# 172 products of the identity with itself, put into TensorE's queue in three places of a two-layer decoder

## The chip, the core and the metric

The kernel runs on one core of a Trainium2 chip. What counts is the device time of one execution in microseconds (us): the median over the runs. A core has a TensorE (matrix products and transposes, called PE in the profile, with PEld for its weight loads), a VectorE (DVE), a ScalarE (ACT), a GpSimd (POOL) and a SyncE (SP), which here issues most of the DMAs. Each engine takes its instructions from a queue of its own, in order; semaphores make one wait for another. TensorE runs at one of two levels, 1.2 or 2.4 GHz; the profile gives the granted clock as a share of the full one, 0.50 or 1.00, and something between for a stretch in which it changed.

## The reference

Two layers over 1024 tokens of width 1024, in float32. Each layer normalizes its input, projects it once into the inputs of four mixers (latent attention, a gated linear recurrence, a diagonal state space model called S5, sparse attention), puts their outputs together, projects, and adds the result to the input. A mixture of 16 experts follows, of which each token uses two:

```
for l in range(DEPTH):
    h = rms_norm(x, mix_norm[l])
    c_q, c_kv, k_pe, lru_x, lru_gate, s5_u, nsa_q, nsa_kv, nsa_gate = jnp.split(h @ w_in[l], IN_SPLITS, axis=-1)
    ...                                   # the four mixers: y_a, y_b, y_c, y_d
    y = rms_norm(jnp.stack([y_a, y_b, y_c, y_d], axis=2), out_norm[l]).reshape(x.shape)
    x = x + y @ w_out[l]
    x = x + hier_moe(rms_norm(x, ffn_norm[l]), ...)   # route, then the experts' gated MLPs

def rms_norm(x, g): return x * rsqrt(mean(x * x, -1) + EPS) * g
```

`hier_moe` picks the best of four groups for a token and the two best of the four experts in it; each expert is `silu(t @ w_gate) * (t @ w_up)` times `w_down`, weighted and summed.

## The kernel before, in words

A matrix product of float32 is made of three products of rounded parts (`mm3`, lines 179 to 183: high by high, high by low, low by high); `hi` (line 169) makes the high part on ScalarE and `lo` (line 177) the low part on VectorE. PSUM, where TensorE writes, has eight banks of 128 x 512 float32; `pt` hands out four of them under names: two called t, one called o, one called x. A bank is given out again when the last reader of its former tile is done.

A layer runs through these stages.

*The norm* (`mixer_norm`). The tokens come in eight tiles of 128. SP loads a tile (line 448) into one of four buffers, of which one holds the gain; so the load of tile i + 3 waits until tile i is read. ScalarE squares and sums it (line 211), GpSimd makes the inverse root (lines 200 and 202), VectorE scales the tile in place (line 454), and TensorE transposes it in eight pieces of 128 x 128 (`T`, line 214), four into bank o and four into bank x. ScalarE and VectorE read each bank as high and low parts (169, 177) into `hT`, which the projection uses.

*The input projection* (`mixer_in`): seven pieces of 128 columns of the weight, each by two halves of 512 tokens, each 24 products of 512 columns, lines 181 to 183. A half needs the norm of its four tiles only. Weights are loaded and split in `wunit` (line 188 and on). In layer 1 the first four weight units are loaded behind the first three tiles.

*Mixers and output projection.* The last stage of it, for the last tile of tokens, uses banks x and o (read by VectorE in line 1510), stores the sum, transposes it and makes the 20 routing logits (line 1533, 20 columns each).

*The routing* (`router`). VectorE finds each token's group and experts (lines 1575 to 1592) and writes them as a 0/1 matrix `Mb`; TensorE turns it into each token's place in its experts' lists (`pos`, 1595 and 1598) and the counts (`cnt`, 1602), two banks t. VectorE copies the counts (1604) and makes the places (1629). Then `moe` starts: `slot_list` (1793 to 1806) finds the tokens of the first expert with 16 small products (line 1796), GpSimd gathers them (1817), TensorE transposes them (`expert_in`). Meanwhile VectorE ranks the experts by count and GpSimd writes a table of slots for all other experts with 16 indirect DMAs (`slot_table`, line 1731), which need the rows that VectorE makes in line 1726.

*The experts* (`moe`): 16 in turn; products with the up weights (into other banks), then with the down weights into banks o and x, and an indirect DMA that adds the result to the layer's output (line 1888). A branch (1936, 1937) runs more tiles if some expert has more tokens than its slots; in these inputs it isn't taken. Layer 1's norm loads what those DMAs have added.

What sets the order: `layer` is a hand-made weave of generators. From its program order, the framework's planner makes one queue for each engine when the kernel is built; it puts an instruction where it reckons that the engine is free and the operands and the bank are there, so that later lines can stand ahead of earlier ones. Nothing crosses the branch of line 1937. At run time each queue is fixed.

The change touches `mixer_norm`, `router` and `layer`, and adds `warm` to the helpers. `identb` is the 128 x 128 identity in bfloat16, made at the start (line 226).

Of the kernel before, what the change touches and what calls it, by code (L numbers as in the profile page):

```python
# [38 lines left out]
def row_bcast(ap, n):  # L39
    return bass.AP(tensor=ap.tensor, offset=ap.offset, ap=[[0, 128], [1, n]])  # L40
# [62 lines left out]
class Trunk:  # L103
# [104 lines left out]
    def meansq(self, src, n, acc, out=None):  # L208
        if out is None:
            out = self.junk()[:src.shape[0], :src.shape[1]]  # L210
        self.nc.scalar.activation(out, src, AF.Square, scale=float(n) ** -0.5, accum_out=acc)

    def T(self, out, in_, k=128):
        self.nc.tensor.transpose(out, in_, self.ident[:k, :k])  # L214
# [221 lines left out]
    def mixer_norm(self, l, src):  # L436

        nc = self.nc
        hTh, hTl = [], []
        for k in range(2):  # L440
            for a, t in (("h", hTh), ("l", hTl)):
                t.append([self.hp.tile([128, 4, 512], F32R, name=f"hT{a}{k}{j}") for j in range(2)])
        self.hT = (hTh, hTl)
        grow = self.p4(name="grow")
        nc.sync.dma_start(grow, row_bcast(self.I["mix_norm"][l], D))
        for i in range(NT):
            xt = self.p4(name="xt")
            nc.sync.dma_start(xt, src[i * 128:(i + 1) * 128, :])
            if i == 2:
                yield  # L450
            ss = self.sm(1, name="ss")
            self.meansq(xt, D, ss, self.p2((128, 1024), BF, name="sqx"))
            r = self.rsqrt(ss, 1)
            nc.vector.scalar_tensor_tensor(xt, xt, r, grow, op0=ALU.mult, op1=ALU.mult)
            for k2 in range(2):
                pt = self.pt("ox"[k2])
                for k in range(4):
                    self.T(pt[:, k * 128:(k + 1) * 128], xt[:, (4 * k2 + k) * 128:(4 * k2 + k + 1) * 128])
                p3 = pt.rearrange("p (k t) -> p k t", k=4)
                ts = slice(128 * (i % 4), 128 * (i % 4) + 128)  # L460
                hh = hTh[i // 4][k2][:, :, ts]
                self.hi(hh, p3)
                self.lo(hTl[i // 4][k2][:, :, ts], p3, hh)
# [1104 lines left out]
    def router(self, l):  # L1568
        nc, v, mp = self.nc, self.nc.vector, self.mp
        self.rtp = None  # L1570
        bc = lambda a, shp, d: a.unsqueeze(d).to_broadcast(shp)
        lg = self.LG[:, :, 0:4]
        le = self.LG[:, :, 4:20].rearrange("p i (g j) -> p i j g", g=4)
        gm = self.rt("gm", 8)
        v.reduce_max(gm, lg, axis=AX.X)
        og = self.first_max(lg, gm, "og")
        big = self.rt("big", 128)
        b4 = big.rearrange("p (i j g) -> p i j g", i=NT, j=4)
        v.tensor_tensor(b4, le, bc(og, [128, NT, 4, 4], 2), op=ALU.mult)
        lx = self.rt("lx").rearrange("p (i j) -> p i j", j=4)  # L1580
        v.reduce_sum(lx, b4, axis=AX.X)
        m1, m2 = self.rt("m1", 8), self.rt("m2", 8)
        v.reduce_max(m1, lx, axis=AX.X)
        o1 = self.first_max(lx, m1, "o1")
        lx2 = self.rt("lx2").rearrange("p (i j) -> p i j", j=4)
        v.scalar_tensor_tensor(lx2, o1, -BIG, lx, op0=ALU.mult, op1=ALU.add)
        v.reduce_max(m2, lx2, axis=AX.X)
        o2 = self.first_max(lx2, m2, "o2")
        o12 = self.rt("o12").rearrange("p (i j) -> p i j", j=4)
        v.tensor_tensor(o12, o1, o2, op=ALU.add)  # L1590
        Mb = mp.tile([128, 128], BF, name="Mb")
        v.tensor_tensor(Mb.rearrange("p (i g j) -> p i g j", i=NT, g=4), bc(og, [128, NT, 4, 4], 3),
                        bc(o12, [128, NT, 4, 4], 2), op=ALU.mult)
        pos, cnt = self.pt(), self.pt()
        nc.tensor.matmul(pos[:, 0:128], self.tri, Mb, start=True, stop=False)
        for i in range(NT - 1):
            n = NT - 1 - i
            nc.tensor.matmul(pos[:, 16 * i + 16:128].rearrange("p (i e) -> p i e", i=n), self.onesb,
                             Mb[:, 16 * i:16 * i + 16].unsqueeze(1).to_broadcast([128, n, 16]),
                             start=False, stop=i == NT - 2)  # L1600
        for i in range(NT):
            nc.tensor.matmul(cnt[:, 0:16], self.onesb, Mb[:, 16 * i:16 * i + 16], start=i == 0, stop=i == NT - 1)
        cn = self.rt("cn", 16)
        v.tensor_copy(cn, cnt[:, 0:16])

        g_ = nc.gpsimd
        t = self.rt("pgt")
        t3 = t.rearrange("p (i g) -> p i g", g=4)
        v.tensor_tensor(t3, lg, bc(gm, [128, NT, 4], 2), op=ALU.subtract)
        nc.scalar.activation(t, t, AF.Exp)  # L1610
        w = [self.rt("w1", 8), self.rt("w2", 8)]
        v.tensor_tensor(w[1], m2, m1, op=ALU.subtract)
        nc.scalar.activation(w[1], w[1], AF.Exp)
        M = []
        for k, o in enumerate((o1, o2)):
            mk = self.rt(f"M{k}", 128)
            g_.tensor_tensor(mk.rearrange("p (i g j) -> p i g j", i=NT, g=4), bc(og, [128, NT, 4, 4], 3),
                             bc(o, [128, NT, 4, 4], 2), op=ALU.mult)
            M.append(mk)
        pg = self.rt("pg", 8)  # L1620
        v.reduce_sum(pg, t3, axis=AX.X)
        den = self.rt("den", 8)
        v.scalar_tensor_tensor(den, w[1], 1.0, pg, op0=ALU.add, op1=ALU.mult)
        v.reciprocal(w[0], den)
        v.tensor_tensor(w[1], w[1], w[0], op=ALU.mult)

        self.PM = mp.tile([128, NT, 16], F32, name="PM")
        PM = self.PM.rearrange("p i e -> p (i e)")
        v.scalar_tensor_tensor(PM, pos[:, 0:128], 1.0, Mb, op0=ALU.add, op1=ALU.mult)
        v.tensor_scalar(PM, PM, -1.0, None, op0=ALU.add)  # L1630

        n = FIXED
        M3 = [m.rearrange("p (i e) -> p i e", e=16)[:, :, 0:n] for m in M]
        WC3, t3 = [self.rt(nm, NT * n).rearrange("p (i e) -> p i e", e=n) for nm in ("WC", "WT")]
        g_.tensor_tensor(WC3, M3[0], bc(w[0], [128, NT, n], 2), op=ALU.mult)
        g_.tensor_tensor(t3, M3[1], bc(w[1], [128, NT, n], 2), op=ALU.mult)
        g_.tensor_tensor(WC3, WC3, t3, op=ALU.add)
        self.split_info(0, n, WC3)

        def rank():  # L1640
            self.slot_table(l, *self.router_rank(cn), cn, M, w)
        return rank
# [311 lines left out]
    def layer(self, l, src):  # L1954
# [15 lines left out]
        if l == 0:  # L1970
            gen = self.s5_gen(0, True)
            next(gen)
        units = self.mixer_in(l)

        norm = self.mixer_norm(l, src)
        next(norm)
# [162 lines left out]
```

## Time and profile before

| | |
|---|---|
| median of 3 runs | 2172.72 us (2164.47 to 2176.85) |
| the profiled execution | 2167.18 us, of it the span of the trace 2165.4 us |
| TensorE (PE) busy | 1846.2 us, 85% of the span, 10386 products |
| weight loads (PEld) | 1508.0 us, 70% |
| VectorE (DVE) | 1309.8 us, 60% |
| ScalarE (ACT) | 1129.7 us, 52% |
| GpSimd (POOL) | 669.0 us, 31% |
| mean granted clock of TensorE | 0.899 |

Products overlap in the pipeline, and the profile counts a product as busy until its result is out; so 85% isn't the share of time in which the array works at its peak. A duration of 390 ns stands for a product of 512 columns whose successor starts 230 ns later. For a price the starts of neighbours are better than durations. The profile's chain of waits is followed back from the end to 1446 us only; it does not reach the first layer or the boundary between the layers. Layer 0 runs to 1117 us, layer 1 from there.

### The profile page before, as it was taken

The numbers are of one execution on the slowest core, as the hardware profiler recorded it, in microseconds if no ns is written. First come the engines' busy times: TensorE is split into PE (matmuls) and PEld (weight loads), VectorE is DVE, ScalarE is ACT, GpSimd is POOL, SyncE is SP. The second block draws the span as 40 slices with busy tenths as digits, with TensorE's granted clock in tenths as the row PEclk, the third lists the DMA queues.
The fourth block names the chain that finished last, engine by engine and source line by source line (L and its number), as shares of the span: only waits on it lengthen the run. The fifth ranks groups of instructions, "written<-read, shape, count | busy, mean of one in ns | idle before, by whom it ended". The sixth has DMA issues, their size and how long they took to land. (4 is left out here: it accounts for less than half of the span.)

```text
span 2165.4 us, 31419 instructions
## 1 busy us (share of the span) xinstructions
PE 1846.2 (85%) x10386; PEld 1508.0 (70%) x10386; DVE 1309.8 (60%) x2895; ACT 1129.7 (52%) x2474; POOL 669.0 (31%) x1130
## 2 busy tenths in 40 slices
PE   4858899999899967888857789989998999689997
PEld 3647876667677766778756678766676777578886
DVE  4976556577655464777725455566776554646664
ACT  4146544466644436565634555455665544357764
POOL 2432453111111126568711224631111111332221
PEclk9979998699889978999978899987999999789999
DMA  7345432113222437898855354311223123489995
GB/s 214 114 109 141 120 120 62 37 53 73 82 81 74 139 129 191 237 259 257 257 129 167 95 132 120 111 59 37 57 69 94 71 81 139 135 239 271 270 273 119
DMA packets 265965, 293.27 MB, mean 135 GB/s; under 512 B 95416, under 2 KB 222264, under 8 KB 265784
## 3 DMA queue, kind: packets, MB, share of 16 engines
q1 hardware_dynamic: 248568, 243.60, 36.7%
q0 software_dynamic: 16640, 46.43, 10.1%
q8 instruction: 87, 1.43, 0.3%
q10 hardware_dynamic: 576, 1.05, 0.1%
q14 instruction: 94, 0.77, 0.1%
HBM read 215.88 MB, written 79.35 MB: 136 GB/s over the span
## 5 line engine op out<-in xcount | busy, mean ns | idle before, releaser
L177 DVE TENSOR_TENSOR wl<-raw,wh 128x512 fp32r<-128x512 f32 (+3 forms) x294 | 214.7, 760 | 99.5 <-ACT wh L169 95.2
L169 ACT ACTIVATE wh<-raw 128x512 fp32r<-128x512 f32 (+3 forms) x294 | 181.9, 658 | 95.2 <-PE ps L182 53.8
L181 PE MATMUL ps<-mo,wh 128*128 128x256 f32 x576 | 171.6, 298 | 24.4 <-ACT mo L169 24.4
L182 PE MATMUL ps<-mo,wh 128*128 128x256 f32 x576 | 167.9, 293 | 0.2 <-DVE mo L177 0.2
L183 PE MATMUL ps<-mo,wl 128*128 128x256 f32 x576 | 166.5, 290 | 0.0
L1201 DVE TENSOR_REDUCE mx<-ps 128x1 f32<-128x640 f32 (+11 forms) x160 | 132.8, 830 | 51.5 <-PE ps L1235 28.7
L181 PEld LDWEIGHTS ps<-mo,wh 128*128 128x128 f32 x576 | 115.7, 201 | 28.5 <-ACT mo L169 28.3
L169 ACT ACTIVATE mo<-ptt 128x512 fp32r<-128x512 f32 x132 | 76.4, 596 | 105.1 <-PE ptt L214 105.1
L177 DVE TENSOR_TENSOR mo<-ptt,mo 128x512 fp32r<-128x512 f32 x132 | 90.5, 686 | 59.6 <-ACT mo L169 59.3
L177 DVE TENSOR_TENSOR ntl<-ptt,at 128x512 fp32r<-128x512 f32 x132 | 89.2, 686 | 56.0 <-ACT at L169 55.4
L1203 ACT ACTIVATE P<-ps,mx 128x640 f32<-128x640 f32 (+7 forms) x128 | 89.0, 698 | 61.2 <-DVE mx L1201 52.1
L169 ACT ACTIVATE at<-ptt 128x512 fp32r<-128x512 f32 x132 | 76.4, 595 | 83.1 <-PE ptt L214 78.8
L182 PEld LDWEIGHTS ps<-mo,wh 128*128 128x128 f32 x576 | 114.9, 200 | 1.4 <-DVE mo L177 0.5
L183 PEld LDWEIGHTS ps<-mo,wl 128*128 128x128 f32 x576 | 114.6, 199 | 0.0
L181 PE MATMUL ptx<-wh,mo 128*128 128x512 f32 x240 | 101.7, 424 | 3.4 <-ACT ch L1147 1.7
L202 POOL TENSOR_TENSOR rr<-rv,mhalf 128x1 f32<-128x1 f32 (+5 forms) x98 | 101.3, 1034 | 7.8
L214 PE MATMUL ptt<-ident,xg 128*128 128x128 f32 x400 | 63.9, 296 | 41.7 <-DMA xg<-hbuf,mo 38.9
L181 PE MATMUL ps<-wh,hT 128*128 128x364 f32 (+1 forms) x256 | 97.8, 383 | 0.0
L183 PE MATMUL ptx<-wh,mo 128*128 128x512 f32 x240 | 96.8, 403 | 0.0
L181 PE MATMUL ps<-hT,wh 128*128 128x512 f32 x224 | 93.1, 417 | 3.8 <-ACT wh L169 3.3
L183 PE MATMUL ps<-hT,wl 128*128 128x512 f32 x224 | 91.1, 411 | 6.0 <-DVE wl L177 4.3
L1817 POOL DMA_INDIRECT xg<-hbuf,mo x50 | 57.1, 1142 | 126.1 <-PE ptt L214 66.0
(636 smaller groups left out, 5811.0 us busy)
## 6 DMA issues: line engine op xcount, KB each, us to landing
raw<-in_moe_w_gate_dram SPq DMA_DIRECT2D x96, 256.0 KB
raw<-in_moe_w_up_dram SPq DMA_DIRECT2D x96, 256.0 KB
mo<-in_moe_w_down_dram SPq DMA_DIRECT2D x32, 512.0 KB
raw<-in_moe_w_down_dram SPq DMA_DIRECT2D x32, 512.0 KB
zm<-mqk SPq DMA_DIRECT2D x16, 512.0 KB
at<-zm SPq DMA_DIRECT2D x16, 512.0 KB
wo<-in_w_out_dram SPq DMA_DIRECT2D x16, 512.0 KB
mo<-yd SPq DMA_DIRECT2D x16, 512.0 KB
```

The costliest lines, as they stand in the source:

```text
L169: self.nc.scalar.activation(out, in_, AF.Copy)
L177: e.tensor_tensor(out, in_, hi.bitcast(F32), op=ALU.subtract)
L181: mm(out, lh, rh, start=start, stop=False)
L182: mm(out, lh, rl, start=False, stop=False)
L183: mm(out, ll, rh, start=False, stop=stop)
L202: g.tensor_tensor(r, v, self.mhalf[:P, 0:1].to_broadcast([P, k]), op=ALU.pow)
L214: self.nc.tensor.transpose(out, in_, self.ident[:k, :k])
L1201: v.tensor_reduce(mx, S3, axis=AX.X, op=ALU.min)
L1203: nc.scalar.activation(P[j][:, 0:n], S3[:, j], AF.Exp, bias=mx[:, j:j + 1], scale=-1.0, accum_out=acc[:, j:j + 1])
L1817: self.nc.gpsimd.indirect_dma_start(out=xg, out_offset=None, in_=self.hbuf[l], in_offset=bass.IndirectOffsetOnAxis(ap=ix, axis=0), bounds_ ...
```

## The change

A helper `warm(bank, n)` issues n products of `identb` with `identb`, repeated four times along the columns (128 x 512 in bfloat16), into a bank. What they write is never read: the norm's transposes write the same bank over, and in the other two places the bank is given back.

Three calls:

- in the norm, two products ahead of each bank's four transposes: eight tiles, two banks, two layers, 64 products;
- in the routing, 24 products into bank o, in the text behind the copy of the counts, in both layers;
- in layer 1, 60 products into a bank t, ahead of the norm.

```diff
+    def warm(self, bank, n=1):
+
+        for _ in range(n):
+            self.nc.tensor.matmul(bank, self.identb, self.identb.unsqueeze(1).to_broadcast([128, 4, 128]),
+                                  start=True, stop=True)
...
             for k2 in range(2):
                 pt = self.pt("ox"[k2])
+                self.warm(pt, 2)
                 for k in range(4):
                     self.T(pt[:, k * 128:(k + 1) * 128], xt[:, (4 * k2 + k) * 128:(4 * k2 + k + 1) * 128])
...
         cn = self.rt("cn", 16)
         v.tensor_copy(cn, cnt[:, 0:16])
+        self.warm(self.pt("o"), 24)
...
         units = self.mixer_in(l)
+        if l:
+            self.warm(self.pt(), 60)
 
         norm = self.mixer_norm(l, src)
```

## Rows read from the trace of the kernel before

**Rows 1.** The page, part 2: granted clock in 40 equal slices of the span, in tenths.

```profile
PEclk9979998699889978999978899987999999789999
```

**Rows 2.** Busy time by stretch (bounds, length, engines' busy us and counts, clock, DMA).

```profile
1141.00:1144.00 3.00, 1.97 (x8) 1.57 (x8) 2.89 (x5) 1.02 (x3) 0.00 (x0) 0.50 0.93 282
...
1146.00:1148.00 2.00, 0.09 (x1) 0.00 (x0) 2.00 (x3) 2.00 (x3) 0.00 (x0) 1.00 0.62 182
...
1155.00:1159.00 4.00, 3.46 (x12) 3.00 (x13) 2.18 (x4) 1.19 (x2) 0.00 (x0) 0.50 0.61 186
...
1160.00:1164.00 4.00, 4.00 (x21) 3.15 (x19) 1.95 (x3) 3.27 (x6) 1.32 (x4) 1.00 0.84 269
...
1168.00:1208.00 40.00, 39.91 (x187) 33.12 (x186) 10.84 (x39) 10.74 (x16) 2.64 (x4) 1.00 0.30 86
```

**Rows 3.** Instructions of line 1937, 1070 to 1140 us: durations (ns), start.

```profile
L1937 PEldq COMPARE_BRANCH  x1: 3442/3442/3442, 1115.9 to 1115.9; - x1
```

**Rows 4.** Order of time, SP's queue, layer boundary: start, length, instruction.

```profile
1127.63 0.35 SPq L445 DMA_DIRECT2D grow<-in_mix_norm_dram  x1
```

**Rows 5.** Order of time, TensorE, layer 1's norm and projection; in brackets: idle before, releaser.

```profile
1136.98 1.11 PE L214 MATMUL pto<-ident,xt 128*128 128x128 f32 x4 [20.42 <-DVE xt L454]
1137.89 1.06 PE L214 MATMUL ptx<-ident,xt 128*128 128x128 f32 x4
1141.68 1.11 PE L214 MATMUL pto<-ident,xt 128*128 128x128 f32 x4 [2.73 <-DVE hT L177]
...
1150.95 1.09 PE L214 MATMUL pto<-ident,xt 128*128 128x128 f32 x4 [4.86 <-DVE xt L454]
...
1158.16 0.63 PE L181 MATMUL ps<-hT,wh 128*128 128x512 f32 x1
1158.59 0.63 PE L182 MATMUL ps<-hT,wh 128*128 128x512 f32 x1
...
1164.85 0.63 PE L214 MATMUL pto<-ident,xt 128*128 128x128 f32 x4 [0.66 <-DVE na L399]
1165.31 0.60 PE L214 MATMUL ptx<-ident,xt 128*128 128x128 f32 x4
...
1167.50 0.66 PE L214 MATMUL pto<-ident,xt 128*128 128x128 f32 x4 [1.12 <-DVE hT L177]
...
1176.02 0.39 PE L182 MATMUL ps<-hT,wh 128*128 128x512 f32 x1
1176.25 0.39 PE L183 MATMUL ps<-hT,wl 128*128 128x512 f32 x1
```

**Rows 6.** Waits of SP's queue, 1105 to 1175 us: total, times, longest.

```profile
SPq L448 <- PE ptx L214: 13.8, 5, 4.6
```

**Rows 7.** Transposes by tile, whole run: durations (ns, least/median/most).

```profile
L214 PE MATMUL pto<-ident,xt x64: 271/421/477, 24.8 to 1167.9; 128*128 128x128 f32 x64
```

**Rows 8.** Order of time, TensorE, around layer 1's routing.

```profile
1827.08 1.96 PE L1533 MATMUL ptx<-mo,hTf 128*128 128x20 f32 x16
...
1851.68 3.60 PE L1533 MATMUL ptx<-mo,hTf 128*128 128x20 f32 x16
1861.15 0.29 PE L1595 MATMUL ptt<-mo,tri 128*128 128x128 bf16 x1 [5.87 <-DVE mo L1592]
...
1863.46 1.10 PE L1796 MATMUL ptt<-mo,mo 128*128 128x6 bf16 x16 [1.43 <-POOL mo L1650]
```

**Rows 9.** Order of time, VectorE, around layer 1's routing.

```profile
1847.46 0.68 DVE L1510 TENSOR_TENSOR xm<-pto,xr 128x512 f32<-128x512 f32 x1
...
1855.48 0.23 DVE L1719 COPY mo<-tokint 128x8 int32<-128x8 int32 x2
1855.62 0.18 DVE L1575 TENSOR_REDUCE rtp<-mo 128x8 f32<-128x32 f32 x1
...
1877.18 0.17 DVE L1726 SCALAR_TENSOR_TENSOR mo<-rtp 128x16 int32<-128x16 f32 x1
```

**Rows 10.** Busy time by stretch, behind layer 0's norm (columns as in rows 2).

```profile
54.00:88.00 34.00, 33.92 (x149) 27.73 (x149) 33.01 (x169) 5.38 (x9) 16.44 (x41) 1.00 0.30 73
```

## The prediction, made before the changed kernel ran

> **What bounds the kernel now.** I read the clock line of the page first [rows 1]: the granted TensorE clock is full in most slices and falls to 0.7 or 0.8 in a few. The change has its places in those: the start of layer 0, the two routings, the start of layer 1. Then I cut layer 1's start into stretches [rows 2], followed TensorE through it in order of time [rows 5], and did the same around the second routing [rows 8, 9].
>
> The reader is to see three things. At the layer boundary TensorE does nothing for 20.42 us and then begins the norm's transposes at the low level [rows 5]. In the norm the engine is not what things wait for: its transposes wait for VectorE, either for the scaled tile (1136.98, 1150.95) or for a bank to be read out (1141.68, 1167.50). The norm's loads in turn wait for transposes, since a tile's buffer is free only behind them: five waits, 13.8 us in all, in layer 1 [rows 6]. Behind the norm TensorE is solid, 39.91 of 40 us at full clock [rows 2], so a microsecond by which the last transposes move is worth a microsecond there. Behind the routing the engine waits 5.87 us for VectorE's choice of experts [rows 8].
>
> **What the change adds.** 60 + 2 x 24 + 64 = 172 products (64: two for each of 16 banks in both layers), nothing removed or moved, no new tile, no DMA. Each product streams 512 columns. No bfloat16 product of that width is in the trace; the nearest rows are the input projection's products of 512 columns, 0.43 us from start to start at the low level (1158.16 to 1158.59) and 0.23 at the high (1176.02 to 1176.25) [rows 5]. I take these two as ends and prices.
>
> *The 60 before layer 1.* TensorE's branch starts at 1115.9 and takes 3.44 us [rows 3], so the products can start at 1119.4 if nothing else holds the engine. In the norm the engine was busy 3.46 of 4 us at the low level in 1155 to 1159 and at the high level in the next stretch [rows 2]; I take as much here: nine at 0.43 and 51 at 0.23, 3.9 + 11.7 = 15.6 us, to 1135.0. Four products of the norm's first two banks bring it to 1135.9. The first transposes start at 1136.98 now: hidden, with 1.1 us to spare. **Term: 0.** The ends: all 60 at 0.23 give 13.8 us, hidden too; all at 0.43 end at 1145.2, and four more at 1146.9, 9.9 us late. If TensorE gets past the branch only when the SP queue issues its first load of the layer, 1127.63 [rows 4], the end is 1127.63 + 16.5 = 1144.1, 7.2 late.
>
> *The two before each bank's transposes.* Four transposes take 0.91 us at the low level (1136.98 to 1137.89) and 0.46 at the high (1164.85 to 1165.31) [rows 5]. So a bank that costs 0.91 now costs 0.46 + 0.46 = 0.92 with its products at the high level, 0.86 + 0.91 = 1.77 if the clock stays low, and where it is high already 0.92 in place of 0.46. Where the transposes wait for the tile and not for the bank, the products lie in that wait, and the bank gains the 0.45.
> Layer 1: tile 0 gains 0.9 and tile 3 gains 0.9 (both wait for the tile); tiles 1 and 2 wait for the bank (1141.68), nothing gained or lost; tile 7 waits for the bank at the high level already, +0.9. In 1155 to 1159, tiles 4 and 5 among the projection's first products, 3.46 us of work at the low level [rows 2] halve, 1.7 gained, but eight norm products stand in it now (1.8). What sets the end is tile 7, whose load waits for tile 4's transposes (buffers three tiles apart) and whose scaling waits for ScalarE and GpSimd: tile 0's and tile 3's gains reach it only in part, and its own +0.9 takes them. **Term: 0**, ends -1.8 (tiles 0 and 3 carry through, tile 7 hidden) and +3.4 (clock low, four banks of tiles 1 and 2 at +0.86).
> Layer 0: the same code; the median transposition into these banks is 421 ns [rows 7], so most of both norms ran at the low level. Here no 60 products stand ahead, so tiles 1 and 2 pay up to 4 x 0.86 = 3.4 until the clock is up, and the tiles and products behind them give most of it back. Behind it VectorE is busy 33.01 of 34 us [rows 10], beside a solid TensorE, and hides part. **Term: +0.5**, ends -1.8 and +3.4.
>
> *The 24 behind the counts.* They need bank o alone, and its last reader ends at 1847.46 + 0.68 = 1848.14 [rows 9], 13 us before the counts (1861.15). The build's planner puts an instruction that is ready into an idle place of its engine's queue, ahead of earlier lines: line 1719, in the slot table, runs at 1855.48, ahead of the routing's first line, 1575, at 1855.62 [rows 9]. So I expect the 24 to stand not behind the counts but in front, in TensorE's gaps between 1848 and 1861. There they have 5.87 us of idle time [rows 8]. 24 at 0.23 are 5.5 us and fit; 24 at 0.43 are 10.3, 4.4 too many. Among the last tile's logits (1851.68, 3.60 us for 16) they would delay these by their own length, or, if they hold the clock up, bring them to the 1.96 us that the same 16 take at 1827.08 [rows 8], and the eight transposes ahead by 0.9: -2.5. I take the gap as filled and only the 16 small products of lines 1595 to 1602 as faster. **Term: -0.3** for each routing, ends -2.5 and +4.4.
>
> **Sum.** 0 + 0 + 0.5 - 0.6 = -0.1 us. The profiled execution has a span of 2165.4 us in 2167.18, 5.5 below the median of the three runs shown, 2172.72; on the median the sum gives 2172.6, and I say 2172. All low ends together give -8.6, all high ends +25.5.
>
> A rule speaks against the change. The Trainium skill, "TensorE: Matmul & The Clock Gate", Part 4 (PE-mode transpose), says that a transposition does not count as busy work and the full clock does not engage for it. The row differs: from 1136.98 to 1146 TensorE did nothing but the norm's transposes, and the clock went from 0.50 in 1141 to 1144 to 1.00 in 1146 to 1148 [rows 2]. By the row the sum is as above; by the rule the two products among four transposes would have to lift the clock alone, and where they can't, the time is that of rival (c), 2179.
>
> **The rivals.**
> (a) *The clock stays up, and the stages follow.* The norms lose their low transposes on the path (tiles 0 and 3: 1.8) and the low work in 1155 to 1159 (1.7), 3.5 for each layer; each routing gains the 2.5 above and holds the clock into the first expert's transposes and products, which I price like the logits' gain, another 1.7. In all 2 x (3.5 + 4.2) = 15.4 us: **2157**. For: low stretches stand at exactly these places [rows 1]. Against: the norm waits for VectorE and for loads, and behind the slot list TensorE waits for the gather, which no clock shortens.
> (b) *Slower: the 24 hold up the slot list.* If they stand where the text has them, between the counts and line 1796, they start where the counts end, 1863.46 - 1.43 = 1862.03 [rows 8], at the low level: nine at 0.43 and fifteen at 0.23, 7.3 us, to 1869.3. The slot list starts at 1863.46 now, so it is 5.8 late, and with it the gather of the first expert's tokens; queued behind VectorE's read of that list are the ranking and line 1726 (1877.18) [rows 9], on which GpSimd's 16 writes of the slot table wait. Twice 5.8 is 11.6: **2184**; all at 0.43, twice 8.9, 2190. It decides from the point where bank o or the planner puts more than four of the 24 behind the counts. For: program order. Against: the early bank and line 1719.
> (c) *Slower: the low clock in the norms.* Two products for four transposes don't hold the high level, and each bank on the path pays 0.86: four in each norm, 6.9 us: **2179**.
> (d) *The 60 are late*, since the branch or a wait holds TensorE until 1127.63: 7.2 us: **2180**. The planner, to which a load may look earlier than it is, could then also reorder ScalarE's and VectorE's queues of that stage, which I can't price.
>
> **How the numbers follow.** My forecast, alone 2162 to 2183 (the three runs shown reach over 12.4 us), has 0.55; (a) 0.18; (b) 0.13; (c) 0.06; (d) 0.08. A new plan for all queues of both layers comes with any added instruction, and with it several us of either sign. The range is 2150 to 2193: (a) and (b) lie in it, with what they can lack by a plan. A measurement of this kernel can tell 0.5%, some 10.9 us, from no change: faster takes (a) and 0.04 of the forecast for a lucky plan, 0.22; slower takes 0.11 of (b), 0.03 of (d) and 0.06 of the forecast for an unlucky one, 0.20; within it 0.58.
>
> **What would show it.** The clock of TensorE at 1.00 when the first transposes of layer 1 start, and their start not later than now, against SP's first load of the layer (9.4 us): the 60 are hidden. Banks of tiles 1 and 2 of that norm at 0.9 us from first product to last transposition: the exchange is even; 1.8: case (c). The 24 ahead of line 1595 and a slot list 2.3 us behind it, as now: no case (b). If the last transposes of layer 1's norm come over 3 us earlier, counted from its first load, or the first expert's transposes run at 0.46 for four, the forecast is too low in gain and (a) holds. A median outside 2162 to 2183 proves the forecast wrong.

## The result, and the profile after

The changed kernel took 2178.59 us in the median of 14 runs (2170.33 to 2193.56) beside 2173.09 us (2151.68 to 2186.67, 14 runs) for the kernel before: ratio 1.0057, 95% interval 1.0030 to 1.0084, or 12.4 us slower (6.5 to 18.3). The ratio is taken over the fast runs alone; the medians as they stand differ by 5.5 us and the means by 10.7, so the sign of the loss is surer than its size. The forecast was no change. The profiled execution took 2173.74 us and its span is 2172.0 us. TensorE's mean clock is 0.914 in it and 0.899 in the profile of the kernel before; over all runs it is 0.913 in the changed kernel's 14 and 0.905 in the 35 runs of the kernel before beside e1. So the products did what they can do: more of the span at the full clock, and a longer span.

The clock line of the page, to be laid beside [rows 1]:

```profile
PEclk9979999899899978999989899977998899799999
```

TensorE in layer 1's norm, in order of time (start, length, instruction; in brackets the idle time before and its releaser). It answers to [rows 5]:

```profile
1109.06 15.90 PE L216 MATMUL ptt<-identb 128*128 128x512 bf16 x60 [3.37 <-PEq L1945]
1124.80 0.59 PE L216 MATMUL pto<-identb 128*128 128x512 bf16 x2
1125.23 0.60 PE L220 MATMUL pto<-ident,xt 128*128 128x128 f32 x4
...
1134.12 1.01 PE L216 MATMUL pto<-identb 128*128 128x512 bf16 x2 [7.42 <-DVE hT L177]
...
1135.79 1.06 PE L216 MATMUL ptx<-identb 128*128 128x512 bf16 x2
...
1143.76 1.01 PE L216 MATMUL pto<-identb 128*128 128x512 bf16 x2 [3.62 <-DVE hT L177]
```

The 60 products take 15.9 us behind the branch and end where tile 0 is ready; tile 0's transposes (1125.23) run at the full clock. Then the engine stands still for 7.42 us. SP's first load of the layer was issued at 1115.35 (1127.63 before, [rows 4]), so tile 1 begins 18.8 us behind it with its products, and 19.6 us with its transposes. Before it was 14.05 us (1141.68 less 1127.63). The clock falls in that gap; these are stretches of the same time (bounds, length, TensorE's busy us and count, clock, DMA share, GB/s), as in [rows 2]:

```profile
1116.00:1126.00 10.00, 10.00 (x50) 1.00 1.01 306
1126.00:1130.00 4.00, 0.70 (x6) 1.00 1.16 278
1130.00:1134.00 4.00, 0.00 (x0) 0.73 0.73 186
1134.00:1138.00 4.00, 3.88 (x14) 0.50 1.01 309
1138.00:1142.00 4.00, 2.12 (x12) 0.92 0.96 331
1142.00:1146.00 4.00, 2.24 (x8) 0.51 0.90 288
```

A bank is free when ScalarE and VectorE have both read it, so their two queues say why TensorE waits. ScalarE after:

```profile
1125.76 1.06 ACT L169 ACTIVATE wh<-raw 128x1024 fp32r<-128x1024 f32 x1 [0.58 <-DMA raw<-in_w_in_dram]
...
1130.96 1.06 ACT L169 ACTIVATE wh<-raw 128x1024 fp32r<-128x1024 f32 x1 [0.54 <-DMA raw<-in_w_in_dram]
1131.93 0.58 ACT L169 ACTIVATE hT<-pto 128x512 fp32r<-128x512 f32 x1
```

ScalarE in the kernel before:

```profile
1138.13 0.60 ACT L169 ACTIVATE hT<-pto 128x512 fp32r<-128x512 f32 x1 [0.69 <-PE pto L214]
1138.63 1.05 ACT L169 ACTIVATE wh<-raw 128x1024 fp32r<-128x1024 f32 x1
1139.57 0.59 ACT L169 ACTIVATE hT<-ptx 128x512 fp32r<-128x512 f32 x1
```

Before, ScalarE reads tile 0's first bank (hT<-pto) 0.69 us after it fell idle, and the casts of the weight pieces (wh<-raw) come between such reads. After, all four casts stand ahead of that read, each waits 0.5 to 0.8 us for its weights' DMA, and a bank that was full at about 1125.8 is read at 1131.93. VectorE, which takes each weight piece's low part (wl<-raw,wh) as it takes a bank's (hT<-pto,hT), reads the bank later still. After:

```profile
1127.64 1.28 DVE L460 SCALAR_TENSOR_TENSOR xt<-xt,rr,grow 128x1024 f32<-128x1024 f32 x1 [0.77 <-POOL rr L202]
1128.85 4.63 DVE L177 TENSOR_TENSOR wl<-raw,wh 128x1024 fp32r<-128x1024 f32 x4
1133.39 0.68 DVE L177 TENSOR_TENSOR hT<-pto,hT 128x512 fp32r<-128x512 f32 x1
```

VectorE in the kernel before:

```profile
1139.74 1.28 DVE L454 SCALAR_TENSOR_TENSOR xt<-xt,rr,grow 128x1024 f32<-128x1024 f32 x1 [0.77 <-POOL rr L202]
1140.94 0.68 DVE L177 TENSOR_TENSOR hT<-pto,hT 128x512 fp32r<-128x512 f32 x1
1141.54 0.68 DVE L177 TENSOR_TENSOR hT<-ptx,hT 128x512 fp32r<-128x512 f32 x1
1142.14 1.22 DVE L177 TENSOR_TENSOR wl<-raw,wh 128x1024 fp32r<-128x1024 f32 x1
```

VectorE's read is the one that releases TensorE. Before, it follows the scaling of the third tile at once; after, the low parts of all four weight pieces stand between, 4.63 us of work without a pause. TensorE's hole grew by as much, from 2.73 us ([rows 5]) to 7.42. Since VectorE is busy from 1127.64 to its read, the trace shows no cost of the casts' waits for DMAs here. The build's planner orders each engine's queue. Its builds (queues alone; of these only 60 was run) fit one reading: it counts the products as TensorE time ahead of tile 0, takes tile 0 to be late, and fills the time with the weight pieces. With 24 products in that place ScalarE's and VectorE's queues keep those pieces where they were, with 32 one cast and one low part stand ahead of the first read, with 40 two, with 60 all four.

The orders of the queues differ between the two kernels in layer 0 up to 170 us and in layer 1's norm and first projection; elsewhere only the added products differ. So the time can be metered in three places, each from a fixed event:
- layer 0: from the first load to ScalarE's second Gelu of the recurrence. In the nine traces here whose layer 0 is untouched, and in the kernel before: 142.6 to 144.1 us.
- routing: from VectorE's last instruction of line 1510 (the last tile's sum; the expectations call it the numbering of the logits) to the point where TensorE's queue turns to the slot list's products, which is the first product of line 1595 ("first count" in the table) plus 0.5 to 0.7 us.
- layer 1: from the first load to the first Gelu. Untouched: 76.8 to 78.0 us; and from the first load to tile 1's transposes, 14.0 to 14.8 us.

| kernel | ratio to before, 95% | layer 0 | routing, layers 0 and 1 | layer 1: tile 0, tile 1 | first Gelu |
|---|---|---|---|---|---|
| before | | 143.5 | 13.8, 14.4 | 9.4, 14.1 | 77.0 |
| changed | 1.0057 (1.0030 to 1.0084) | 149.1 | 16.9, 14.2 | 9.9, 19.6 | 84.1 |
| changed, second profile (e14) | | 146.9 | 14.2, 16.9 | 9.4, 19.5 | 84.9 |
| e1 only the 60 | 1.0039 (1.0012 to 1.0067) | 144.1 | 14.1, 12.5 | 10.4, 19.6 | 81.6 |
| e2 only the 24 | 1.0034 (1.0008 to 1.0059) | 142.8 | 16.9, 14.2 | 9.4, 14.1 | 77.5 |
| e3 only the norm's pairs | 1.0035 (1.0003 to 1.0067) | 147.6 | 14.0, 14.0 | 9.4, 14.9 | 79.2 |
| e4 casts first, no product | 1.0025 (0.9999 to 1.0051) | 142.6 | 13.8, 14.5 | 9.9, 19.7 | 82.8 |
| e5 the 60, in order | 1.0032 (1.0006 to 1.0058) | 144.0 | 14.5, 14.3 | 10.1, 14.8 | 77.1 |
| e6 that order, no product | 0.9997 (0.9976 to 1.0019) | 143.3 | 14.3, 14.2 | 9.6, 14.3 | 77.0 |
| e7 the 24 in the gap | 1.0054 (1.0028 to 1.0080) | 143.3 | 15.4, 14.1 | 9.3, 14.0 | 77.0 |
| e8 the 24 behind the counts | 1.0013 (0.9991 to 1.0034) | 143.2 | 13.3, 13.8 to the first count | 9.5, 14.2 | 77.4 |
| e9 before, unchanged | 1.0017 (0.9989 to 1.0044) | 142.8 | 14.0, 12.4 | 10.0, 14.7 | 78.0 |
| e10 as e7 | 1.0042 (1.0010 to 1.0074) | 143.8 | 15.3, 15.3 | 10.1, 14.8 | 78.0 |
| e11 one per bank | 0.9982 (0.9948 to 1.0015) | 139.6 | 13.9, 13.9 | 9.5, 14.6 | 78.2 |
| e12 all, in order | 1.0031 (1.0000 to 1.0063) | 147.0 | 13.7, 12.3 | 13.9, 16.3 | 82.2 |
| e13 one per bank, layer 0 | 0.9997 (0.9965 to 1.0029) | 140.5 | 13.9, 14.3 | 9.4, 14.1 | 76.8 |
| e15 as e12, second profile | | 146.4 | 12.3, 13.9 | 13.9, 16.3 | 82.6 |

By these meters the changed kernel lost 5.6 + 2.9 + 7.0 = 15.5 us in its first profile and 3.3 + 2.9 + 7.9 = 14.1 us in its second (routing as the sum over both layers: 31.1 in both, 28.2 before). Both lie within the measured 6.5 to 18.3 us, so nothing beside these three places is needed. It is not shown that nothing else counts: SP's first load of layer 1 comes 12.3 us earlier in the changed kernel's profile than in that of the kernel before, and 9.0 us earlier in e6, whose layer 0 is that of the kernel before, so the stretches between the meters differ by several us from one execution to the next.

Nor does every metered loss last. At the first product of line 1113, in layer 0's latent attention, the changed kernel's two profiles stand at 345.7 and 347.2 us and the kernel before at 344.8 (the ten with layer 0 untouched at 342.0 to 345.5). Of the 5.6 and 3.3 us, 0.8 and 2.4 are left there, and with these the sums are 10.7 and 13.2 us. Layer 1's loss lasts: from its first load to its first product of that line it is 305.0 and 307.4 us, where the seven profiles with layer 1 untouched have 296.5 to 300.1.

The ratios of the parts are no better than a few us either: e1, e2 and e3 add up to 1.0108, the whole is 1.0057, and the kernel before beside itself (e9) has 1.0017.

### The profile page after: what moved, and what is told of

Read it like the earlier page. It is cut to its first block, busy times and chain, and to the rows that moved or that the text cites. A ratio compares the mean times of both kernels' runs of the same rounds, so it can differ in the third digit from the quotient of the medians.

```text
span 2172.0 us, 31758 instructions
## 1 busy us (share of the span) xinstructions
PE 1875.3 (86%) x10558; PEld 1512.3 (70%) x10558; DVE 1304.6 (60%) x2895; ACT 1131.2 (52%) x2474; POOL 667.7 (31%) x1130
## 3 DMA queue, kind: packets, MB, share of 16 engines
q0 software_dynamic: 16640, 46.43, 10.1%
## 5 line engine op out<-in xcount | busy, mean ns | idle before, releaser
L181 PEld LDWEIGHTS ps<-mo,wh 128*128 128x128 f32 x576 | 115.9, 201 | 28.7 <-ACT mo L169 28.5
L182 PE MATMUL ptx<-wl,mo 128*128 128x512 f32 x240 | 95.6, 398 | 0.0
```

Of the source, the lines that this page charges most:

```text
L181: mm(out, lh, rh, start=start, stop=False)
L182: mm(out, lh, rl, start=False, stop=False)
```

## The experiments

The theory (A in the expectations): most of the loss is the order of the queues that the planner makes around the products, above all the weights' casts and low parts ahead of tile 0's reads. The main rival (B): it is the length of the products themselves. The cuts show lines of each edit, some left out (...): of e1, e2, e3, e5, e11, e12 and e13 against the changed kernel, of e4, e6, e7 and e8 against the kernel before.

**e1, only the 60.**

```
-                self.warm(pt, 2)
...
-        self.warm(self.pt("o"), 24)
```

> Only the 60 products between the layers; the norm's pairs and the routing's 24 are gone. Meter: from the layer's first load (the norm's row) to ScalarE's first Gelu of layer 1, 77.0 us in the kernel before and 84.1 in the changed one. Theory A (order): the 60 make the planner put the four weight casts ahead of ScalarE's and VectorE's reads of tile 0, as in the changed kernel, and that is the loss: 83 to 85 us on the meter, ratio to before 1.003. Theory B (the products' own time, the norm's pairs above all): the 60 are hidden, so 77 us and ratio 1.000.

Ratio 1.0039, tile 1 at 19.6 us as in the changed kernel, first Gelu at 81.6, short of the 83 to 85 that A expected. ScalarE's and VectorE's queues have the four weight pieces ahead of tile 0's reads here too. B is out as the whole of this part: without a pair or one of the 24, 4.6 of the 7.0 us are there. The pairs alone (e3) give 2.2 more, 6.8 together.

**e2, only the 24.**

```
-                self.warm(pt, 2)
...
-        if l:
-            self.warm(self.pt(), 60)
```

> Only the 24 products behind each routing's counts. No other queue's order differs from the kernel before. Meter: from VectorE's last numbering of experts' logits (line 1510 of before) to the slot list, 13.8 and 14.4 us before in layers 0 and 1, 16.9 and 14.2 in the changed kernel. Theory A: the 24 lie in TensorE's gaps ahead of the counts and cost nothing, 13.5 to 14.5 us in both and ratio 1.000; the 16.9 of layer 0 is then chance or the stage ahead. Theory C: the 24 hold the counts of layer 0 up: 16.9 us again in layer 0, ratio 1.0015.

16.9 us in layer 0, 14.2 in layer 1: theory A was wrong in this part, C was right. The order of all other queues is that of the kernel before, so the 24 alone do it. The ratio, 1.0034, is above the 2.9 us of the meters (1.0013), which its interval holds. How is read from the changed kernel's second profile (e14), where the same two values come in the other layer.

**e3, only the pairs of the norm.**

```
-        self.warm(self.pt("o"), 24)
...
-        if l:
-            self.warm(self.pt(), 60)
```

> Only the two products ahead of each bank of four transposes in the norms of both layers. Layer 1: ScalarE's queue keeps tile 0's read ahead of the casts here. Theory A: layer 1's meter (first load to first Gelu) stays at 77 +-2 us; layer 0's (first load to the second Gelu, 143.5 us before, 149.1 in the changed kernel) goes to 147 to 150, since layer 0's queues are ordered anew as in the changed kernel; ratio 1.002. Theory B (eight banks of tiles 1 to 7 pay 0.9 us each on the path): layer 1's meter 83 to 85 as in the changed kernel, ratio 1.005.

Layer 0 147.6 us (+4.1), as A has it; layer 1 79.2, 2.2 above before, a little past what A allowed (79) and far from B's 83 to 85. Layer 0's norm itself became 1.5 us longer: VectorE's last read of a bank ends at 56.61 us here and at 55.11 before. The other 2.6 us come in the S5 stage behind it, whose queues are ordered anew; that the order makes them is argued, since no run has it without the products.

**e4, the order alone.** No product at all; the loads of tiles 0 to 2 and the four weight pieces are written ahead of tile 0's reads, and those are made to depend on the last cast:

```
+                if l and i == k2 == 0:
+                    yield
...
+                if l and i == k2 == 0:
+                    self.after(a, self.cast[0])
+                    self.after(b, self.cast[1])
```

> The kernel before with no product added; in layer 1 alone the norm's first three loads and the four first weight pieces are written ahead of tile 0's reads, and a dependence puts ScalarE's and VectorE's reads of tile 0's first bank behind the last of the four casts, as the changed kernel's queues have it. Theory A: the order alone costs it, first load to first Gelu 83 to 86 us (77.0 before), TensorE idle 5 us or more between the first and the second tile's transposes, ratio 1.003. Theory B: 77 +-2 us, ratio 1.000.

TensorE in e4, in order of time; no product of the change is in it:

```profile
1128.01 1.12 PE L213 MATMUL pto<-ident,xt 128*128 128x128 f32 x4 [20.98 <-DVE xt L462]
1128.92 1.06 PE L213 MATMUL ptx<-ident,xt 128*128 128x128 f32 x4
1137.87 1.12 PE L213 MATMUL pto<-ident,xt 128*128 128x128 f32 x4 [7.88 <-DVE hT L177]
```

The same hole (7.88 us, released by VectorE's read of the bank), tile 1 at 19.7 us and the first Gelu at 82.8: 5.7 us of loss by the order alone, in the stage (83 to 86 us expected, 77 by B). The edit holds ScalarE's and VectorE's reads together, so it does not tell the two queues apart. The ratio, 1.0025, agrees in size, but its interval just touches 1; the stage is the proof.

**e5, the 60 alone with the casts behind tile 0**, and **e6, that order without the 60.** `gate` is ScalarE's and VectorE's read of tile 0's second bank:

```
+        if self.gate:
+            self.after(ia, self.gate[0])
+            self.after(ib, self.gate[1])
```

> The 60 products alone, with one dependence more: in layer 1 the casts of the four first weight pieces stand behind ScalarE's and VectorE's reads of tile 0's two banks. Theory A (order): the second tile's transposes come 14 us behind the first load or earlier (14.05 before, 19.6 with the 60 alone), first load to first Gelu 75 to 78 us (77.0 before, 81.6 with the 60 alone), ratio 1.000 +-0.002. Rival D (the 60 themselves hold the second tile up, by TensorE or by a bank): 19 to 20 us and 81 to 82 us as with the 60 alone.

> The same dependence without any product, to tell what the 60 do in a given order. Theory A: the order sets the meter: 75 to 78 us, within 1 us of the kernel with the 60 in this order; if the full clock at tile 0 is worth anything, the kernel with the 60 is shorter than this one by up to 2 us (0.9 for tile 0, 0.9 for tile 3). Ratio 0.999 +-0.002.

TensorE in e5:

```profile
1123.41 14.80 PE L220 MATMUL ptt<-identb 128*128 128x512 bf16 x60 [3.32 <-PEq L1949]
1139.92 0.66 PE L224 MATMUL pto<-ident,xt 128*128 128x128 f32 x4 [1.71 <-DVE xt L464]
1140.41 0.60 PE L224 MATMUL ptx<-ident,xt 128*128 128x128 f32 x4
1144.61 1.11 PE L224 MATMUL pto<-ident,xt 128*128 128x128 f32 x4 [3.60 <-DVE hT L178]
```

The hole is 3.60 us, tile 1 is at 14.8 us (14 expected) and the first Gelu at 77.1, with all 60 products in place: rival D is out, and the order is the cause. e6 has 77.0 without any product: the full clock at tile 0 in e5 (0.49 us from one bank's transposes to the other's, 0.91 before) is worth nothing at the first Gelu, against the 2 us that I allowed. e5's ratio, 1.0032, is above what A expected. Its meters give 0.1 us in layer 1 and 0.5 in the routings; where the rest would lie isn't shown.

**e7, the 24 between the logits and the counts**, and **e10**, the same again.

```
+            if behind and j == 0:
+                self.after(m, behind)
...
-        self.warm(self.pt("o"), 24)
+        self.warm(self.pt("o"), 24, self.last)
```

> Only the 24, and the first of them held behind the last tile's logits, so that none stands among the logits any more; all 24 fall between the logits and the counts. Last numbering of experts' logits (line 1510 of before) to slot list in layer 0: 13.8 us before, 16.9 with 5 + 2 of the 24 among the transposes and the logits. Theory C' (those seven, 2.3 + 0.8 us, are the loss): VectorE's read of the last logits is back at 7.3 us behind line 1510 (10.6 with them), and the slot list comes at 14 to 16.2 us, since the 24 now overrun the gap of 5.87 us by up to 2.4 us. Rival E (a clock that fell by chance in layer 0): the logits stay late, 16.9 us.

> The 24 held behind the last logits, once more, byte for byte. By its stages (slot list 1.5 us late in layer 0, 0.3 early in layer 1) the ratio is 1.0006; the first run gave 1.0054. If that was chance, now 1.000 to 1.003; if something outside the two stages pays 10 us for the 24, again 1.004 to 1.006, and the profile has to show where.

TensorE in e7, layer 0:

```profile
771.93 3.60 PE L1541 MATMUL ptx<-mo,hTf 128*128 128x20 f32 x16
775.37 7.83 PE L216 MATMUL pto<-identb 128*128 128x512 bf16 x24
783.04 0.22 PE L1603 MATMUL ptt<-mo,tri 128*128 128x128 bf16 x1
```

The logits are undivided and as long as before (3.60 us, [rows 8]); the 24 start behind them, take 7.8 us and overrun the gap, so the meter is at 15.3 to 15.4 us in three of four routings. C' holds in the stage. The two ratios, 1.0054 and 1.0042, are higher than 1.3 and 2.4 us by the meters explain (1.0006 and 1.0011); the second interval holds the meters' value, the first doesn't. That stays open; e9, the unchanged kernel, has 1.0017.

**e8, the 24 behind the counts**, the case that the prediction called (b):

> Only the 24, held behind the last product of the counts, where the text has them: the case that the prediction called (b) and priced at 5.8 us for each routing. Last line 1510 to the slot list's products: line 1595 as before (13.1 us), the slot list's own products (line 1796) 7 to 9 us behind line 1595 where they stand 2.3 us behind it before; ratio 1.004 to 1.006. If TensorE reaches them before GpSimd's list is ready (1.4 us idle there now), 1.4 us of them is hidden.

In layer 0 the first product of line 1595 starts at 778.36 and the slot list's first product at 786.69, 8.3 us behind it and 6.0 more than before, as (b) priced it (5.8). The first expert's transposes begin 28.5 us behind line 1510, 23.3 before. Yet the ratio is 1.0013: VectorE's queue is planned anew, GpSimd's first write of the slot table comes 26.8 us behind line 1510 in place of 30.3, and in the expert loop the same instructions, laid beside those of the kernel before, stand some 3.4 us earlier than they did ahead of the routing, in both layers. So here a delay that was priced at one wait was paid back by the plan that came with it.

**e9, the kernel before against itself.**

> The kernel before, unchanged, timed against itself: what no change looks like. Every theory expects 1.000 and the stages as before (layer 1 first load to first Gelu 77.0 us, line 1510 to slot list 13.8 and 14.4 us). A ratio off by more than 0.002, or an interval that leaves 1.000 out, would say that the ratios of the small edits (1.0054 for the 24 in the gap, whose stages give +1.3 us) hold more chance than their intervals tell.

Ratio 1.0017, within its interval of 1, the stages as before. But at one place the trace falls 6.7 us behind the first profile of the same kernel. Stretches of layer 1's sparse attention, in the first profile of the kernel before:

```profile
1645.00:1650.00 5.00, 2.77 (x10) 0.50 0.08 18
1650.00:1655.00 5.00, 5.00 (x26) 0.90 0.56 151
1655.00:1660.00 5.00, 5.00 (x27) 1.00 0.23 85
```

and in e9, where the same work begins 4 us earlier:

```profile
1641.00:1646.00 5.00, 2.85 (x12) 0.50 0.07 18
1646.00:1651.00 5.00, 5.00 (x15) 0.50 0.47 147
1651.00:1656.00 5.00, 5.00 (x19) 0.50 0.23 89
1656.00:1661.00 5.00, 5.00 (x17) 0.50 0.00 0
1661.00:1666.00 5.00, 4.98 (x23) 0.81 0.00 0
```

The same instructions, and the engine solid in both; the clock rises in the first of the solid stretches in one and in the fourth in the other. An event like this is one source of the spread of the runs, which is over 1%, and the reason why the stages and not the ratios carry the proofs here.

**e11, one product ahead of each bank in both layers**, and **e13, in layer 0 alone.**

```
-                self.warm(pt, 2)
+                self.warm(pt, 1)
```

> Only the norm's products, one ahead of each bank in place of two. Theory A (what the pairs cost is the new order of the queues behind the norm in layer 0, not their length): half the products don't give half the loss; layer 0's norm ends 1 to 2 us earlier than in the kernel before on VectorE, as with two, and the second Gelu of layer 0 (143.5 us before, 147.6 with two) lands anywhere in 141 to 149, by the order. Theory B (length): half of the loss, 145.5 us, and layer 1's first Gelu at 78.1 (77.0 before, 79.2 with two). Ratio 1.001 to 1.003 by either.

> One product ahead of each bank of the norm in layer 0 alone; layer 1 and the routing as before. Layer 0's queues are those of the run with one per bank in both layers, whose second Gelu came 3.9 us before the kernel before's. Theory A: again 139 to 140.5 us there (143.5 before), layer 1's first Gelu 77 to 78 us from its first load, ratio 0.998, which would make it the fastest of all kernels here. Theory B (the 3.9 us were chance): 143 us and 1.000.

Half the products give a gain of 3.9 us at layer 0's second Gelu where two gave a loss of 4.1. That is not a length. The norm's last bank is read at 54.07 us (55.11 before), and the rest comes behind it; the new order is what is left to explain it, and no run has that order without the products. With layer 1 untouched (e13) the gain is 3.0 us there and the ratio 0.9997. The gain is still there at line 1113 (339.8 and 337.7 us, 342.0 to 345.5 untouched), but it can't be told from nothing in the whole.

**e12, all three parts, casts behind tile 0, and 14 products in the gap in place of 24**, and **e15**, the same again.

> All three parts of the change, with layer 1's casts behind the reads of tile 0 and the routing's products held behind the last logits, 14 in place of 24 so that they fit the 5.87 us of idle time. Theory A: layer 1's first Gelu at 77 to 79.5 us from the first load (84.1 in the changed kernel), slot list 13.4 to 14.4 us behind line 1510 in both layers, layer 0's second Gelu still at 147 to 149 us, which nothing here mends: ratio to before 1.002 to 1.003, 6 to 8 us below the changed kernel's 1.0057. Theory B (length of the products): layer 1 stays at 82 us or more, ratio 1.005.

> All three parts in order once more: TensorE stood still for 5.31 us between the first and the second of the 60 in the first run, with nothing in the profile that it waited for, and layer 1's first transposes came 13.9 us behind the first load. If that belongs to this program, again 13.5 to 14.2 us and a first Gelu at 82 us; if it was chance, 9.9 to 10.4 us and 77.5 to 79.5 us.

The routing is mended: 12.3 to 13.9 us, the first value being that of the kernel before where its logits ran at the full clock (e1 and e9, 12.5 and 12.4). Layer 0 is not, as expected. Layer 1 is at 82.2 us where I expected 77 to 79.5. B's 82 or more is met in number, but not by B's cause: tile 1 follows tile 0 by 2.4 us (9.7 in the changed kernel), and tile 0 itself is late, by a cause that I did not know. TensorE in e12:

```profile
1115.23 0.38 PE L220 MATMUL ptt<-identb 128*128 128x512 bf16 x1 [3.21 <-PEq L1953]
1120.91 15.72 PE L220 MATMUL ptt<-identb 128*128 128x512 bf16 x59 [5.31 <-issue]
...
1136.90 0.60 PE L226 MATMUL pto<-ident,xt 128*128 128x128 f32 x4
```

After the first of the 60 TensorE stands still for 5.31 us and waits for nothing that the profile shows. The 60 then end at 1136.6, and tile 0 is 4 us late. The second profile has it again (4.99 us), so it belongs to this program; the changed kernel, e1 and e5 have none. The queues of instruction loads move one packet in the stall's last 2.4 us (queue, kind: packets, MB, share):

```profile
q8 instruction: 1, 0.02, 2.8%
```

The changed kernel, e5 and e15 have such a packet too, 5.5 to 6.5 us behind the one at the branch; in e5 (about 1120, then 1126.5) the products run meanwhile. So the reading is that in e12 the code loaded at the branch ends right behind the first product. That is an inference from two traces. The Trainium skill, "Runtime: NRT & Kernel Launch", section Instruction fetch mechanics, says that code is fetched ahead in blocks, in sequence, and that a taken branch whose target isn't held makes the engine wait for the fetch. The traces are in line with it and do not prove it: 3.2 to 3.5 us idle at the branch in all of them, and 5 us once more in these two.

**e14, the changed kernel again, one execution.**

> The changed kernel once more, for its stages alone. If they belong to the kernel and not to chance: layer 0's second Gelu at 148 to 150 us, slot list of layer 0 16.4 to 17.2 us behind line 1510, layer 1's first Gelu 83.5 to 85.5 us from the first load. Any of them back at the kernel before's value (143.5, 13.8, 77.0) drops out of the account.

Layer 1's loss recurs (84.9). Layer 0's is smaller than expected (146.9), and the 16.9 us of the routing moved from layer 0, where it was expected, to layer 1: it belongs to the 24, not to one layer. (The one time of this execution, 2196.48 us, is no comparison.) TensorE in e14, layer 0:

```profile
777.09 2.14 PE L216 MATMUL pto<-identb 128*128 128x512 bf16 x5
779.06 0.96 PE L1540 MATMUL ptx<-mo,hTf 128*128 128x20 f32 x8
779.87 0.59 PE L216 MATMUL pto<-identb 128*128 128x512 bf16 x2
780.30 0.96 PE L1540 MATMUL ptx<-mo,hTf 128*128 128x20 f32 x8
```

and layer 1, the same program in the same execution:

```profile
1870.67 2.34 PE L216 MATMUL pto<-identb 128*128 128x512 bf16 x5
1872.80 1.73 PE L1540 MATMUL ptx<-mo,hTf 128*128 128x20 f32 x8
1874.37 1.02 PE L216 MATMUL pto<-identb 128*128 128x512 bf16 x2
1875.18 1.73 PE L1540 MATMUL ptx<-mo,hTf 128*128 128x20 f32 x8
```

Seven of the 24 stand ahead of and among the last tile's logits. Where the clock rises during the five, the halves of the logits take 0.96 us and win back what the seven cost; where it doesn't, they take 1.73 us and the seven cost 3 us. Of six such routings (changed, e2, e14) three are at 16.9 and three at 14.2 us; of the eighteen without any of the 24 (before, e1, e3 to e6, e9, e11, e13) none is over 14.6.

## Why the prediction was wrong

The median, 2178.59 us, lies within the 2162 to 2183 that I gave the forecast, and close to the 2179 and 2180 of (c) and (d). The first says only how wide that band is: the kernel before has 2173.09 us beside it, and the ratio's interval lies above 1. The second is chance, as the parts show.

**The 60, term 0.** Their own time was right: 15.9 us (15.6 forecast), behind a branch of 3.84 us, 6.3 us ahead of SP's first load, so rival (d)'s hold at the branch did not occur; tile 0 starts 9.9 and 9.4 us behind that load, 9.35 before. The step that failed is the one that the prediction wrote down and left without a price: "The planner, to which a load may look earlier than it is, could then also reorder ScalarE's and VectorE's queues of that stage". The term 0 took every other queue to keep its order. The planner did reorder, and by its builds not for the reason given: it took tile 0 for late, not the load for early. Four low parts of weights, 4.6 us, came ahead of VectorE's read of tile 0. The stage lost 7.0 and 7.9 us at the first Gelu; e4 shows 5.7 of it without a product, and e5 shows 0.1 with the 60 and the casts behind tile 0's reads.

**Layer 1's pairs, term 0.** The exchange was not even. Tile 1's bank took 1.67 us (1134.12 to 1135.79), near the 1.8 that I named for case (c). The clock had fallen in the 7.42 us in which the engine did nothing; but the pairs don't hold it without that hole either. In e12 it is 1.00 from 1136 to 1142 and 0.50 from 1144 to 1150, with only short waits between:

```profile
1142.06 0.59 PE L220 MATMUL pto<-identb 128*128 128x512 bf16 x2 [1.20 <-DVE hT L178]
...
1143.79 1.01 PE L220 MATMUL ptx<-identb 128*128 128x512 bf16 x2 [0.70 <-DVE hT L178]
```

So (c)'s condition came true, at a smaller price: e3, with the pairs alone, has +2.2 us, within the ends of -1.8 and +3.4, where (c) has four banks at 0.86.

The prediction also set the rise of the clock under transposes alone, in the kernel before, against a rule. It does not come in every execution: in e9, the same kernel, the same transposes run from 1134.84 on at 0.50, and the clock is still at 0.50 in 1150 to 1155, among the projection's products.

**Layer 0, term +0.5.** The norm's own +1.5 us (e3) lies within the ends. The further 2.6 us (e3), and 5.6 and 3.3 in the changed kernel altogether, come behind the norm, with the new order, which I counted only as "several us of either sign" around the whole; at line 1113, 0.8 and 2.4 us of these two are left. With one product per bank the sign turned (e11, e13): the range could hold this, no step of the sum could.

**The routings, term -0.3 each.** The place was right: the 24 stand ahead of the counts. "I take the gap as filled" was wrong: the planner put five and two of them behind the last transposes and among the logits, the case that I had named ("Among the last tile's logits") and not taken. Measured: +2.9 over both layers, in one of the two each time.

**The rivals.** (b)'s price was right and its time wrong (e8: +6.0 us at the slot list, ratio 1.0013). (a) did not come: no metered stage of the changed kernel is shorter by more than 0.2 us. (d)'s hold did not come, and (c)'s price did not. The common fault is that I priced instructions in the order in which the kernel before had them.

## What to carry to other kernels

Where a planner orders the queues, an instruction that costs nothing on its engine is still an input to the plan of all the others: lay the new queues beside the old first, and price the first wait that the new order makes, above all long work that now stands ahead of the read that frees a bank. Filler for the clock must not stand among work that something waits for: pin it behind the last such instruction and size it to the gap (14 in place of 24 in e12 cost the routing nothing). And with a time that runs over 1% from one execution to the next, prove a part by a fixed stage of the trace, in two profiles, rather than by the whole, and see whether the loss still stands some stages on.

## What the runs showed of the hardware

- The granted clock can stay at 0.50 under solid work: in e9 for some 15 us (1646 to 1661), where another run of the same kernel had 0.90 in the first 5 us. That trace fell 6.7 us behind there. The Trainium skill, "TensorE: Matmul & The Clock Gate", Part 1, says that the rise differs from run to run of one kernel; these traces agree, though this rise came much later than in the other run.
- The same transposes of the norm can see the clock rise or not: in the kernel before it went from 0.50 in 1141 to 1144 to 1.00 in 1146 to 1148 [rows 2]; in e9, the same kernel, it stayed at 0.50 (1134 to 1155).
- A bfloat16 product of 512 columns takes 0.43 us from start to start at the low level and 0.22 at the high (the 24 of e7 hold both), as the float32 rows had it (0.43 and 0.23, [rows 5]).
- The 60 products behind the same branch, in another program, can stall TensorE for 5.0 to 5.3 us right behind the first of them (e12, e15) or not at all (e5).
